# Products for the meta tokens over 128 rows, with meta tiles that are cleared once, in a hybrid retention and latent-attention encoder block

## The chip, the cores and the metric

The kernel runs on one core of a Trainium2 chip. The metric is the device time of one execution in microseconds (us). A time is quoted as the median of several executions; the profile is that of one further execution, whose own time is given beside it. The engines are TensorE (PE: its matrix products; PEld: its weight loads), VectorE (DVE), ScalarE (ACT), GpSimd (POOL) and SyncE (SP), whose queue issues all the DMAs that this text speaks of.

## The reference

16 learned meta tokens are put ahead of 1024 tokens of width 1024. One layer follows: a mixer with two branches, retention (8 heads, both directions, chunks of 128) and latent attention (8 heads, bidirectional softmax over all 1040 keys), then a dense SwiGLU network. At the end the meta positions are dropped, so that they matter only as keys, values and the first state of a scan. Cut to the two places where they enter:

```python
# retention, per head; the meta tokens fill the last 16 rows of the first chunk of 128
incr = jnp.einsum('bnjhd,jh,bnjhe->nbhde', kc, w_k, vc)       # state that a chunk adds
cross = jnp.einsum('bnihd,ih,nbhde->bnihe', qc, w_q, states_prev)
...
# attention, per head, over keys of 1024 tokens and 16 meta tokens
s = jnp.einsum('bqhd,bkhd->bhqk', qn, k_nope) + jnp.einsum('bqhr,bkr->bhqk', qr, k_rope)
p = jax.nn.softmax(s.astype(jnp.float32) * scale, axis=-1).astype(v.dtype)
return jnp.einsum('bhqk,bkhd->bqhd', p, v)
```

## The kernel before

All is float32. Where a product must be exact enough, an operand is split into a high and a low part (a cast and a subtraction), and three products high x high, low x high, high x low are added; line 137 to 139 (`mm3`) and line 217 are these products. Large projections use seven instead of eight block products (`seven`, line 185 on): a block of weights is loaded by SP, combined on POOL, cast on ACT (L209) and its low part made on DVE (L210), and used on PE (L217).

The program runs through these stages: the input projections with retention woven into them (retention lies between 300 and 520 us); the latent projections; the retention branch's output projection, whose last tiles (`ret_out`) are multiplied by gates that were stored earlier (load at L853, product at L854, store at L855); attention (from 693 to 985 us); the merge and the SwiGLU network.

The source is not the order of execution. The kernel is written straight through, and a scheduler with a timeline of its own moves instructions within each engine's queue, by what they depend on and by when a buffer comes free. A tile in on-chip memory lies at the next free address of a stack of pools. So a tile of another size shifts all later tiles of its pool and of the pools above, they then lie over other old tiles, and their first writes wait for other readers.

**Retention** (`core_pair`, `core`): for each of 8 heads the state that the meta tokens leave is one product, L651: the stationary operand `km` has 16 rows and 64 columns, the moving one, `vm`, 16 rows and 128 columns. It is in float32 and runs as two instructions. `km` is made once for a pair of heads (load L623, scaling on ACT at L625), `vm` is loaded for each head (L635). It lies between products of 128 rows.

**Attention** works on 32 units, each 256 queries of one head. A unit's scores (L137 to L139, 96 rows) go to DVE (L995) and ACT (the exponential, L997). Its probabilities are then turned on PE (L1005: 128x128, four to a bank) and written as high part `pth` (ACT, L1007) and low part `ptl` (DVE, L1008). The 16 meta keys are turned by L1013. Their high part goes to rows 0 to 15 and their low part to rows 32 to 47 of a ninth block of `pth` (L1016 on ACT, L1017 on DVE); before that POOL clears rows 0 to 47 of that block, in every unit (L1015). The tile `vt` of values holds the matching rows of the meta values, cleared once (L934). The unit's output is 16 products of 128 rows (L1035) and one of 48 rows for the meta keys (L1036). The output of a unit is worked out during the next unit, and `pth` and `ptl` have two buffers each. Between L1036 and the next unit's scores PE mostly has four or eight turns (L1005).

Before attention's first scores can run, its queries and keys are loaded (L951 to L954), and the weights `vr` of the values (L129, 512 KB), split into `vh` and `vl` (L132 on ACT, L133 on DVE), multiply the latent keys into `vt`: nine blocks of six products, shown as `o<-vh,ckh` and the like, each block evacuated by ACT (L1076) and DVE (L1077) through one of two PSUM tiles.

Of the kernel before, what the change touches and what calls it, by code (L numbers as in the profile page):

```python
# [10 lines left out]
F32R = mybir.dt.float32r  # L11
# [37 lines left out]
def build(nc, tc, A, out):  # L49
# [4 lines left out]
    def mk(pl, shape, tag, dt=F32):  # L54
        count[0] += 1
        name = f"{tag}_{count[0]}"
        n = int(np.prod(shape[1:]))
        if n % LINE == 0:
            return pl.tile(list(shape), dt, tag=tag, name=name)
        t = pl.tile([shape[0], -(-n // LINE) * LINE], dt, tag=tag, name=name)[:, :n]  # L60
        return t if len(shape) == 2 else t.rearrange("p (a b) -> p a b", b=shape[2])
# [4 lines left out]
    def sb(ctx, name, bufs=1, side=None, space=None):  # L66
        kw = {"reuse_waits": "tile"}
        if side:
            kw["side"] = side
        if space is not None:  # L70
            kw["space"] = space
            if space == DRAM:
                kw = {"space": space}
        return ctx.enter_context(tc.tile_pool(name=name, bufs=bufs, **kw))
# [177 lines left out]
    with ExitStack() as c1:  # L252
# [347 lines left out]


        cw = sb(cc, "core", 1)
        ay = sb(cc, "ay", 6)

        def core_pair(p):
            rq, rk = mk(cw, (P, S), "rq"), mk(cw, (P, S), "rk")
            load(rk, qk_d[1, p])
            load(rq, qk_d[0, p])
            kw = mk(cw, (P, NB, 2, P), "kw")
            km = mk(cw, (NM, 2, 64), "km")  # L610
            tf, tbk = mk(cw, (P, P), "tf"), mk(cw, (P, P), "tbk")
            load(tf, t_d[8 + p])
            load(tbk, t_d[12 + p])
            for g in range(2):
                ps = mk(pc, (P, 512), "mm").rearrange("p (c i) -> p c i", i=P)
                for c in range(4):
                    pe.transpose(ps[:, c, :], rk[:, (4 * g + c) * P : (4 * g + c + 1) * P], ident)
                for h in range(2):
                    hh = 2 * p + h
                    src = ps[:, :, h * 64 : h * 64 + 64]  # L620
                    act.mul(kw[:, 4 * g : 4 * g + 4, h, 0:64], src, kwf[:, hh : hh + 1])
                    dve.tensor_scalar(kw[:, 4 * g : 4 * g + 4, h, 64:128], src, kwb[:, hh : hh + 1], None, ALU.mult)
            load(km, km_d[p // 2, :, (p % 2) * P : (p % 2) * P + P].rearrange("t (h c) -> t h c", c=64))  # L623
            for h in range(2):
                act.mul(km[:, h, :], km[:, h, :], kwm[:NM, 2 * p + h : 2 * p + h + 1])  # L625
            return rq, rk, kw, km, tf, tbk

        def core(p, h, rq, rk, kw, km, tf, tbk):
            hh = 2 * p + h
            dmat = mk(cw, (P, P), "dmat")  # L630
            load(dmat, t_d[hh])
            hs = slice(h * 64, h * 64 + 64)
            v, vm = mk(cw, (P, NB, P), "v"), mk(cw, (NM, P), "vm")
            load(v, v_d[hh].rearrange("p (c e) -> p c e", e=P))
            load(vm, vm_d[hh])  # L635
            qw = mk(cw, (P, NB, P), "qw")
            rq3 = rq[hs].rearrange("p (c i) -> p c i", i=P)
            pool.tensor_mul(qw[0:64], rq3, tf[hs].unsqueeze(1).broadcast_to([64, NB, P]))
# [291 lines left out]
    with ExitStack() as c1:  # L930
        qk = sb(c1, "qk", 3)
        vp = sb(c1, "v", 1)
        vt = mk(vp, (P, NB + 1, H, P), "vt", F32R)
        pool.memset(f(vt)[0:48, NB], 0.0)  # L934
        ps_s = sb(c1, "ps_s", NS, space=PSUM)
        ps_o = sb(c1, "ps_o", NO, space=PSUM)
        ps_t = sb(c1, "ps_t", NT, space=PSUM)
# [72 lines left out]
        def turn_meta(prs, pt):  # L1010
            tm = mk(ps_t, (P, 4, P), "t")
            for s in range(2):
                pe.transpose(tm[:NM, s, :], prs[s][:, S:L], ident)  # L1013
            tmf = tm[:NM, 0:2, :].rearrange("p s i -> p (s i)")
            pool.memset(f(pt[0])[0:48, NB, :], 0.0)  # L1015
            act.copy(pt[0][:NM, NB, :], tmf)  # L1016
            dve.tensor_sub(pt[0][32:48, NB, :], tmf, f(pt[0])[:NM, NB, :])  # L1017

        def inverse(hh, qc, sums):
            sm = mk(w4, (P, 2), "sm")  # L1020
# [10 lines left out]
        def mix_values(hh, qc, pt, lb):  # L1031
            po = mk(ps_o, (P, 512), "o")
            for b in range(NB):
                for j in range(2):
                    pe.matmul(po[:, :256], vt[:, b, hh, :], pt[j][:, b, :], start=(b == 0 and j == 0), stop=False)  # L1035
            pe.matmul(po[:, :256], vt[0:48, NB, hh, :], pt[0][0:48, NB, :], start=False, stop=True)  # L1036
            ta, tb_ = mk(w2, (64, 256), "oa"), mk(w2, (64, 256), "ob")
            act.copy(ta, po[64:128, :256])
            act.copy(tb_, po[0:64, :256])
            pool.tensor_add(ta, ta, tb_)  # L1040
            hs = slice((hh % 2) * 64, (hh % 2) * 64 + 64)
            c = slice(qc * 256, qc * 256 + 256)
            if hh < H - 2:
                pool.tensor_mul(ta, ta, lb)
                store(o_d[hh // 2, hs, c], ta)
            else:
                pool.tensor_mul(o3[qc // 2][hs, (qc % 2) * 256 : (qc % 2) * 256 + 256], ta, lb)
# [40 lines left out]

        for i, (hh, qc) in enumerate(units):
            nxt = units[i + 1] if i + 1 < len(units) else None  # L1090
            pt = [mk(ptp, (P, NB + 1 - j, 256), t, F32R) for j, t in enumerate(("pth", "ptl"))]
            p = hh // 2
            if hh % 2 == 1 and p < 3:
                if qc == 0:
# [356 lines left out]
```

## Time and profile before

| what | value |
|---|---|
| time, median of 3 | 1789.69 us (1787.7 to 1791.53) |
| the profiled execution's own time, and its span | 1783.0 us, 1781.2 us |
| granted TensorE clock, mean | 0.989 |
| PE products, busy | 1718.1 us, 96% of the span |
| DVE, ACT, POOL busy | 1346.5, 861.8, 798.4 us |
| attention's product for the meta keys (L1036) | 32 instructions |
| clearing of the meta block (L1015, POOL) | 32 of 305 ns each |
| retention's product for the meta tokens (L651) | 16 instructions (8 products) |

A row of a timeline reads: start in us from the beginning of the span, duration in us, engine, line, operation, what it writes and reads, its shape (for a product rows*columns of the stationary operand and then the moving operand, rows x columns), and how many instructions the row merges; in brackets, the engine's idle time before it and what ended it. Products are pipelined and their ends are modelled, so the distance between two starts, not the duration, is what a product costs in a dense stream. A row of a view by stages reads: stretch, its length, and for PE, PEld, DVE, ACT and POOL the busy time with the number of instructions; then the granted clock, the DMA engines' share and GB/s.

### The profile page before, as it was taken

The page shows a single profiled execution, that of the slowest core. Times are in us where ns is not written, and L with a number is a line of the kernel's source. Part 1 is how long each engine was busy: PE and PEld are TensorE (multiplying, and loading weights), DVE is VectorE, ACT ScalarE, POOL GpSimd, SP SyncE. Part 2 cuts the span into 40 slices and gives each one's busy share as a digit, 9 for nine tenths or more (in the row PEclk, how much of TensorE's full clock was granted, in tenths as well). Part 3 has the DMA queues.
Part 4 walks back from the last instruction along what each step waited for, and adds up shares of the span by engine and source line. Part 5 has one row for each costly group of instructions (what it writes and reads, how often), then busy time and mean ns, then how long its engine had stood idle before and what let it go on. Part 6 is the DMA issues. An engine that isn't in the chain of part 4 may idle for free.

```text
span 1781.2 us, 26455 instructions
## 1 busy us (share of the span) xinstructions
PE 1718.1 (96%) x8804; PEld 1440.9 (81%) x8804; DVE 1346.5 (76%) x2448; ACT 861.8 (48%) x1614; POOL 798.4 (45%) x633
## 2 busy tenths in 40 slices
PE   8999999999998898999999999899999999999997
PEld 6788777888887687899998888788888888787787
DVE  8846778888788767787878657767766666987965
ACT  7425766343434524677788345432333332543435
POOL 2322267575654321234332524666677656523422
PEclk9999999999999899999999999999999999999999
DMA  7734824465647784111112745233323333854512
GB/s 260 239 103 136 284 84 136 159 225 190 209 137 250 229 292 138 28 34 40 30 51 63 244 172 164 79 101 107 112 95 101 107 101 105 281 175 129 154 57 95
DMA packets 145434, 253.60 MB, mean 142 GB/s; under 512 B 18889, under 2 KB 36738, under 8 KB 145298
## 3 DMA queue, kind: packets, MB, share of 16 engines
q1 hardware_dynamic: 145298, 251.92, 43.3%
q8 instruction: 69, 1.13, 0.3%
q14 instruction: 67, 0.55, 0.1%
HBM read 174.93 MB, written 76.85 MB: 141 GB/s over the span
## 4 chain that ended last, share of the span: by engine, by line
PE 53%; DVE 7%; DMA 3%; issue 2%; ACT 2%; SPq 0%; POOL 0%; DVEq 0%; ACTq 0%; POOLq 0%
PE mm L217 33%; PE o L1035 3%; PE mm L137 3%; PE mm L138 3%; PE mm L139 3%; PE t L1005 3%; DVE slot L154 1%; PE s L137 1%; PE s L138 1%; PE s L139 1%; DMA slot<-g_d 1%; DVE ptl L1008 1%; DVE slot L210 1%; DVE pr L995 1%; PE o L138 1%
## 5 line engine op out<-in xcount | busy, mean ns | idle before, releaser
L217 PE MATMUL mm<-slot,slot 128*128 128x512 f32 x2604 | 596.1, 390 | 9.1 <-DVE slot L210 4.0
L217 PEld LDWEIGHTS mm<-slot,slot 128*128 128x128 f32 x2604 | 488.5, 188 | 115.6 <-DVE slot L210 7.0
L209 ACT CAST slot<-slot 128x512 fp32r<-128x512 f32 (+1 forms) x413 | 246.1, 597 | 453.1 <-PE mm L217 367.9
L210 DVE TENSOR_TENSOR slot<-slot,slot 128x512 fp32r<-128x512 f32 (+1 forms) x413 | 370.4, 898 | 71.8 <-ACT slot L209 70.8
L217 PE MATMUL mm<-ht,slot 128*128 128x512 f32 x648 | 219.1, 399 | 6.9 <-DVE slot L210 3.4
L191 POOL TENSOR_TENSOR slot<-slot,slot 128x512 f32<-128x512 f32 (+1 forms) x61 | 86.7, 1421 | 218.9 <-DMA slot<-in_w_in 52.9
L217 PE MATMUL mm<-h,slot 128*128 128x512 f32 x536 | 184.5, 403 | 0.0
L207 POOL TENSOR_TENSOR slot<-slot,slot 128x512 f32<-128x512 f32 (+1 forms) x61 | 83.9, 1377 | 182.2 <-DVE slot L210 169.8
L217 PEld LDWEIGHTS mm<-ht,slot 128*128 128x128 f32 x648 | 122.0, 189 | 34.5 <-DVE slot L210 5.1
L154 DVE TENSOR_TENSOR slot<-slot,slot 128x512 fp32r<-128x512 f32 x137 | 116.2, 862 | 17.9 <-ACT slot L153 17.2
L217 PE MATMUL mm<-lt,slot 128*128 128x512 f32 x324 | 128.3, 396 | 0.0
L192 POOL TENSOR_TENSOR slot<-slot,slot 128x512 f32<-128x512 f32 (+1 forms) x61 | 85.3, 1399 | 75.9 <-DVE slot L210 71.2
L217 PEld LDWEIGHTS mm<-h,slot 128*128 128x128 f32 x536 | 101.2, 190 | 21.7 <-DVE slot L210 0.6
L153 ACT CAST slot<-slot 128x512 fp32r<-128x512 f32 x137 | 83.3, 620 | 73.1 <-DMA slot<-f_d 29.6
L995 DVE TENSOR_SCALAR_CACHE_REDUCE pr<-s,sq_c 128x384 f32<-128x384 f32 (+1 forms) x192 | 103.2, 573 | 8.3 <-PE t L1013 5.4
L217 PE MATMUL mm<-l,slot 128*128 128x512 f32 x268 | 106.6, 398 | 0.0
L139 PE MATMUL mm<-slot,slot 128*128 128x512 f32 (+1 forms) x288 | 105.4, 366 | 0.0
L138 PE MATMUL mm<-slot,slot 128*128 128x512 f32 (+1 forms) x288 | 105.3, 366 | 0.0
L137 PE MATMUL mm<-slot,slot 128*128 128x512 f32 (+1 forms) x288 | 105.2, 367 | 0.0
L1008 DVE TENSOR_TENSOR ptl<-t,pth 128x512 fp32r<-128x512 f32 x128 | 85.7, 685 | 20.0 <-ACT pth L1007 19.2
L193 POOL TENSOR_TENSOR slot<-slot,slot 128x512 f32<-128x512 f32 (+1 forms) x61 | 90.1, 1477 | 1.4
L1007 ACT CAST pth<-t 128x512 fp32r<-128x512 f32 x128 | 71.8, 580 | 25.5 <-PE t L1005 25.2
(363 smaller groups left out, 3463.2 us busy)
## 6 DMA issues: line engine op xcount, KB each, us to landing
slot<-in_w_in SPq DMA_DIRECT2D x106, 256.0 KB
f_d<-slot SPq DMA_DIRECT2D x71, 256.0 KB
slot<-f_d SPq DMA_DIRECT2D x71, 256.0 KB
slot<-in_xT SPq DMA_DIRECT2D x48, 256.0 KB
slot<-z_d SPq DMA_DIRECT2D x44, 256.0 KB
slot<-in_w_g SPq DMA_DIRECT2D x44, 256.0 KB
slot<-in_w_u SPq DMA_DIRECT2D x44, 256.0 KB
slot<-in_w_dq SPq DMA_DIRECT2D x48, 192.0 KB
```

The lines of the kernel that those rows point to most:

```text
L137: pe.matmul(ps, sh, mh, start=start, stop=False)
L138: pe.matmul(ps, sh, ml, start=False, stop=False)
L139: pe.matmul(ps, sl, mh, start=False, stop=stop)
L154: dve.tensor_sub(lo, t, f(hi))
L191: pool.tensor_add(s1, a21, a22)
L192: pool.tensor_sub(s2, s1, a11)
L193: pool.tensor_sub(a21, a21, a11)
L209: act.copy(hi, side[b])
L210: dve.tensor_sub(low, side[b], f(hi))
L217: pe.matmul(ps, sw[:, ks], sx, start=begins and q == qs[0] and i == 0, stop=q == nq - 1 and i == 2, skip_group_check=True)
L995: dve.tensor_scalar(pr[:, c], ps[:, :n], sq_c[:, qb : qb + 1], None, ALU.mult, ALU.max, accum_out=mx[:, j : j + 1])
L1008: dve.tensor_sub(pt[1][d], tp, f(pt[0])[d])
```

## The change

In retention, `km` and `vm` become tiles of 128 rows that are made once, ahead of all heads, and cleared by POOL. Loads and scaling still write their first 16 rows; L651 reads all 128. In attention, the ninth block of `pth` goes away. Two tiles `ptm0` and `ptm1` of 128 rows by 256 columns take its place; they are cleared once, are used in turn by even and odd units, and only their rows 0 to 15 and 32 to 47 are rewritten. The clearing in every unit is gone, `vt` is cleared over 128 rows instead of 48, and L1036 reads 128 rows. The added rows are zero in both operands. `pth` shrinks by the 1 KB per partition of its ninth block in each of its two buffers, and the two new tiles take as much at an earlier place in the stack.

```diff
--- before.py
+++ after.py
@@ -600,6 +600,10 @@
 
 
         cw = sb(cc, "core", 1)
+
+        km, vm = mk(cw, (P, 2, 64), "km"), mk(cw, (P, P), "vm")
+        pool.memset(km, 0.0)
+        pool.memset(vm, 0.0)
         ay = sb(cc, "ay", 6)
 
         def core_pair(p):
@@ -607,7 +611,6 @@
             load(rk, qk_d[1, p])
             load(rq, qk_d[0, p])
             kw = mk(cw, (P, NB, 2, P), "kw")
-            km = mk(cw, (NM, 2, 64), "km")
             tf, tbk = mk(cw, (P, P), "tf"), mk(cw, (P, P), "tbk")
             load(tf, t_d[8 + p])
             load(tbk, t_d[12 + p])
@@ -620,19 +623,19 @@
                     src = ps[:, :, h * 64 : h * 64 + 64]
                     act.mul(kw[:, 4 * g : 4 * g + 4, h, 0:64], src, kwf[:, hh : hh + 1])
                     dve.tensor_scalar(kw[:, 4 * g : 4 * g + 4, h, 64:128], src, kwb[:, hh : hh + 1], None, ALU.mult)
-            load(km, km_d[p // 2, :, (p % 2) * P : (p % 2) * P + P].rearrange("t (h c) -> t h c", c=64))
+            load(km[:NM], km_d[p // 2, :, (p % 2) * P : (p % 2) * P + P].rearrange("t (h c) -> t h c", c=64))
             for h in range(2):
-                act.mul(km[:, h, :], km[:, h, :], kwm[:NM, 2 * p + h : 2 * p + h + 1])
-            return rq, rk, kw, km, tf, tbk
-
-        def core(p, h, rq, rk, kw, km, tf, tbk):
+                act.mul(km[:NM, h, :], km[:NM, h, :], kwm[:NM, 2 * p + h : 2 * p + h + 1])
+            return rq, rk, kw, tf, tbk
+
+        def core(p, h, rq, rk, kw, tf, tbk):
             hh = 2 * p + h
             dmat = mk(cw, (P, P), "dmat")
             load(dmat, t_d[hh])
             hs = slice(h * 64, h * 64 + 64)
-            v, vm = mk(cw, (P, NB, P), "v"), mk(cw, (NM, P), "vm")
+            v = mk(cw, (P, NB, P), "v")
             load(v, v_d[hh].rearrange("p (c e) -> p c e", e=P))
-            load(vm, vm_d[hh])
+            load(vm[:NM], vm_d[hh])
             qw = mk(cw, (P, NB, P), "qw")
             rq3 = rq[hs].rearrange("p (c i) -> p c i", i=P)
             pool.tensor_mul(qw[0:64], rq3, tf[hs].unsqueeze(1).broadcast_to([64, NB, P]))
@@ -931,7 +934,11 @@
         qk = sb(c1, "qk", 3)
         vp = sb(c1, "v", 1)
         vt = mk(vp, (P, NB + 1, H, P), "vt", F32R)
-        pool.memset(f(vt)[0:48, NB], 0.0)
+        pool.memset(f(vt)[:, NB], 0.0)
+
+        ptm = [mk(vp, (P, 256), f"ptm{i}", F32R) for i in range(2)]
+        for t in ptm:
+            pool.memset(f(t), 0.0)
         ps_s = sb(c1, "ps_s", NS, space=PSUM)
         ps_o = sb(c1, "ps_o", NO, space=PSUM)
         ps_t = sb(c1, "ps_t", NT, space=PSUM)
@@ -1012,9 +1019,8 @@
             for s in range(2):
                 pe.transpose(tm[:NM, s, :], prs[s][:, S:L], ident)
             tmf = tm[:NM, 0:2, :].rearrange("p s i -> p (s i)")
-            pool.memset(f(pt[0])[0:48, NB, :], 0.0)
-            act.copy(pt[0][:NM, NB, :], tmf)
-            dve.tensor_sub(pt[0][32:48, NB, :], tmf, f(pt[0])[:NM, NB, :])
+            act.copy(pt[2][:NM], tmf)
+            dve.tensor_sub(pt[2][32:48], tmf, f(pt[2])[:NM])
 
         def inverse(hh, qc, sums):
             sm = mk(w4, (P, 2), "sm")
@@ -1033,7 +1039,7 @@
             for b in range(NB):
                 for j in range(2):
                     pe.matmul(po[:, :256], vt[:, b, hh, :], pt[j][:, b, :], start=(b == 0 and j == 0), stop=False)
-            pe.matmul(po[:, :256], vt[0:48, NB, hh, :], pt[0][0:48, NB, :], start=False, stop=True)
+            pe.matmul(po[:, :256], vt[:, NB, hh, :], pt[2], start=False, stop=True)
             ta, tb_ = mk(w2, (64, 256), "oa"), mk(w2, (64, 256), "ob")
             act.copy(ta, po[64:128, :256])
             act.copy(tb_, po[0:64, :256])
@@ -1088,7 +1094,7 @@
 
         for i, (hh, qc) in enumerate(units):
             nxt = units[i + 1] if i + 1 < len(units) else None
-            pt = [mk(ptp, (P, NB + 1 - j, 256), t, F32R) for j, t in enumerate(("pth", "ptl"))]
+            pt = [mk(ptp, (P, NB, 256), t, F32R) for t in ("pth", "ptl")] + [ptm[i % 2]]
             p = hh // 2
             if hh % 2 == 1 and p < 3:
                 if qc == 0:
```

In the changed kernel lines from 604 on have numbers that are higher by 3 to 7. The new tiles lie below the pool that first holds `vr`, `vh` and `vl`, so these lie 2048 bytes higher than before. That is where the change moves instructions; elsewhere the order of PE, ACT, DVE and SP stays what it was, but for a pair of neighbouring DMAs in retention and one in attention.

On SP's queue, before, the load of `vr` stands behind the loads of keys and queries of the first two heads (`k`, `q`):

```order
L954 DMA q_1444_6939<-qr_1283_6148 16x1024
L951 DMA k_1447_6942<-kr_613_3038 16x1040
L952 DMA k_1447_6942<-kr_613_3038 16x1040
L954 DMA q_1445_6940<-qr_1282_6147 16x1024
L954 DMA q_1445_6940<-qr_1284_6149 16x1024
L129 DMA vr_7082<-in_w_uv 128x1024
L951 DMA k_1600_7609<-kr_612_3037 16x1040
```

On SP's queue in the changed kernel (L856, L858, L899 and L900 are the old L853, L855, L896 and L897) it stands ahead of the last stores and loads of the gated tiles:

```order
L899 DMA qr_1271_6138<-slot_6680 128x512
L129 DMA vr_7078<-in_w_uv 128x1024
L858 DMA r_d_82<-slot_6706 128x512
L900 DMA qr_1272_6139<-slot_6679 128x512
L856 DMA slot_6807<-g_d_84 128x512
L899 DMA qr_1273_6140<-slot_6711 128x512
```

So the load moves up by 28 places. Its wait is now for a product that reads `slot_6737`, the first of the last `seven`.

On ACT, at the last casts of the output projection's weights, before:

```order
L233 COPY slot_6741<-mm_6743 128x512
L894 CAST slot_6719<-slot_6718 128x512
L209 CAST slot_6862<-slot_6737 128x512
L967 CAST k_1442_6929<-kf_6958 64x384
L967 CAST k_1446_6941<-kf_6962 64x384
L132 CAST kh_7603<-kr_7601 128x256
```

and on ACT in the changed kernel (L897 is the old L894, L974 the old L967):

```order
L233 COPY slot_6733<-mm_6735 128x512
L132 CAST vh_7080<-vr_7078 128x1024
L897 CAST slot_6711<-slot_6710 128x512
L209 CAST slot_6854<-slot_6729 128x512
L132 CAST kh_7595<-kr_7593 128x256
L974 CAST k_1434_6925<-kf_6954 64x384
```

The cast to `vh` now stands ahead of the last cast of the output projection's weights. On DVE the subtraction that makes `vl` likewise moves up, to between L234 and L235 of that last `seven`, and two L966 move behind the L854 that they led.

On PE, ahead of the first scores (`s`), before:

```order
L138 MATMUL t_6996<-cql_1274_6129,qh_6917 128x384
L139 MATMUL t_6996<-cqh_1273_6128,ql_6918 128x384
L137 MATMUL s_7042<-k_1442_6929,q_1440_6927 128x384
L137 MATMUL s_7047<-k_1442_6929,q_1440_6927 128x384
L137 MATMUL t_7010<-cqh_1269_6124,qh_6917 128x384
```

and on PE in the changed kernel, from the last of the first six value products on:

```order
L139 MATMUL o_7084<-vh_7080,ckl_1268_6125 128x512
L137 MATMUL o_7093<-vh_7080,ckh_1265_6122 128x512
L138 MATMUL o_7093<-vl_7081,ckh_1265_6122 128x512
L139 MATMUL o_7093<-vh_7080,ckl_1266_6123 128x512
L137 MATMUL o_7093<-vh_7080,ckh_1267_6124 128x512
L138 MATMUL o_7093<-vl_7081,ckh_1267_6124 128x512
L139 MATMUL o_7093<-vh_7080,ckl_1268_6125 128x512
L137 MATMUL s_7038<-k_1434_6925,q_1432_6923 128x384
L137 MATMUL s_7043<-k_1434_6925,q_1432_6923 128x384
```

Twelve value products (two of the nine blocks) have moved from behind the first scores to ahead of them.

## The prediction

> **What bounds the kernel now.** I read the page's first part, then the busy times by stage, then timelines of PE at the places that the change touches.
>
> ```profile
> PE 1718.1 (96%) x8804; PEld 1440.9 (81%) x8804; DVE 1346.5 (76%) x2448; ACT 861.8 (48%) x1614; POOL 798.4 (45%) x633
> 300.00:520.00 220.00, 218.15 (x1223) 183.60 (x1224) 183.61 (x437) 83.99 (x148) 142.99 (x95) 1.00 0.60 194
> 680.00:700.00 20.00, 14.03 (x63) 12.74 (x61) 10.50 (x19) 5.83 (x13) 6.34 (x7) 0.83 0.61 177
> 740.00:985.00 245.00, 240.55 (x1713) 222.64 (x1712) 200.20 (x601) 190.33 (x419) 85.55 (x124) 1.00 0.17 47
> ```
>
> PE is the bound. In retention it is idle for 1.85 of 220 us, in attention for 4.45 of 245 us, and DVE, the next, is busy for 83% and 82% of them. So what PE saves there, the kernel saves, until PE has to wait for DVE or ACT. POOL is busy for 35% of attention. The stretch between the two is another matter: from 680 to 700 us PE is idle for 6 us and its granted clock is 0.83.
>
> **Attention's meta product.** The distance between starts is what a product costs. One unit's last products, with the meta product of 48 rows:
>
> ```profile
> 795.46 0.28 PE L1035 MATMUL o<-ptl,vt 128*128 128x256 f32 x1
> 795.67 0.38 PE L1036 MATMUL o<-pth,vt 48*128 48x256 f32 x1
> 795.98 0.66 PE L1005 MATMUL t<-ident,pr 128*128 128x128 f32 x4
> 796.39 0.43 PE L137 MATMUL s<-k,q 96*128 96x384 f32 x1
> ```
>
> The same transition elsewhere, without it:
>
> ```profile
> 808.14 0.28 PE L1035 MATMUL o<-pth,vt 128*128 128x256 f32 x1
> 808.26 0.60 PE L1005 MATMUL t<-ident,pr 128*128 128x128 f32 x4
> 808.61 0.42 PE L137 MATMUL o<-ckh,kh 128*128 128x384 f32 x1
> ```
>
> With it: 796.39 - 795.46 = 0.93 us from the last L1035 to the scores (first fence). Without (second): 808.61 - 808.14 = 0.47 us. A product of 128 rows and 256 columns adds 808.26 - 808.14 = 0.12 us, so one of the usual form would make 0.59. The meta product costs 0.93 - 0.59 = 0.34 us more than its form with 128 rows: it starts 0.09 late, the turns after it 0.19, and the turns take 0.06 longer. Is it the row count? Products of 96 rows show nothing of the kind:
>
> ```profile
> 799.76 0.28 PE L1035 MATMUL o<-pth,vt 128*128 128x256 f32 x1
> 799.87 0.34 PE L137 MATMUL s<-k,q 96*128 96x384 f32 x1
> 800.05 0.33 PE L138 MATMUL s<-k,q 96*128 96x384 f32 x1
> ```
>
> 0.11 us into them, 0.18 us for 384 columns. After the change L1036 has exactly the form of L1035, so I price it at 0.12 us. 32 units x 0.34 = 10.9 us. Of this I take 95%, 10.3 us, since 1.8% of the stage is idle already and a faster PE meets DVE (82% busy, and 85% when 10 us are gone) a little more often. Bounds: 80%, 8.7 us, and the full 10.9.
>
> [...]
>
> The rows of L1036 wait for a cast of ACT, and what it waits for changes:
>
> ```profile
> 799.61 0.36 ACT L1016 CAST pth<-t 16x256 fp32r<-16x256 f32 x1
> L1015 POOL MEMSET pth<- x32: 302/305/306, 721.7 to 970.2; 48x256 f32 x32
> ```
>
> 32 clearings of 305 ns go, 9.8 us of POOL. POOL is 35% busy here, so I price this at nothing on the end; two clearings of a tile, `vt`'s larger one and retention's two take under 3 us of POOL by the same row (cost goes by columns: 256 take 0.3), under POOL's idle time. The cast now waits for the meta product of two units earlier to have read the tile. The meta product that ends at 796.05 is that of the unit before the cast's, so even it leaves 799.61 - 796.05 = 3.6 us, and the one that matters lies a unit further back, (970.2 - 721.7) / 31 = 8.0 us by the clearings: 11 us in all. I price it at nothing; if that cover went, every 0.1 us of wait would be 3.2 us over 32 units.
>
> **Retention's meta product.** The same comparison, two instructions of 16 rows and 64 columns against two of the same type with 128 rows and columns:
>
> ```profile
> 314.71 0.39 PE L217 MATMUL mm<-ht,slot 128*128 128x512 f32 x1
> 315.03 0.43 PE L651 MATMUL mm<-vm,km 16*64 16x128 f32 x2
> 315.39 0.50 PE L217 MATMUL mm<-h,slot 128*128 128x512 f32 x1
> ...
> 498.48 0.40 PE L217 MATMUL mm<-l,slot 128*128 128x512 f32 x1
> 498.71 0.38 PE L670 MATMUL mm<-st,qw 128*128 128x128 f32 x2
> 498.85 0.71 PE L217 MATMUL mm<-h,slot 128*128 128x512 f32 x2
> ```
>
> And one of few columns:
>
> ```profile
> 806.90 0.33 PE L139 MATMUL o<-ckh,kl 128*128 128x384 f32 x1
> 807.08 0.38 PE L1013 MATMUL t<-ident,pr 128*16 128x128 f32 x2
> 807.21 0.37 PE L1035 MATMUL o<-ptl,vt 128*128 128x256 f32 x1
> ```
>
> From the product ahead to the one behind it is 0.68 us against 0.37, so 0.31 us for each of 8 heads, 2.5 us. Here 64 columns stay, which no row of 128 rows shows. The nearest, 16 columns at 807.08, starts 0.18 us after a product of 384 columns, as any does, and lets the next one start after 0.13. So few columns alone cost nothing there; I take 2.4 us, and bound it by 0 and 2.5. POOL's two clearings of 128 columns stand ahead of the first head's products on POOL, and the first load of `km` waits for one of them: under 0.6 us, on engines that are not the bound.
>
> [...]
>
> **The way into attention.** By the order, `vr` is loaded 28 DMAs earlier, `vh` and `vl` are made earlier, and twelve value products move ahead of the first scores. What is there now:
>
> ```profile
> 686.65 0.34 PE L139 MATMUL t<-cqh,ql 128*128 128x384 f32 x1
> 692.85 0.98 PE L137 MATMUL s<-k,q 96*128 96x384 f32 x2 [5.87 <-DMA q<-qr]
> 693.63 0.52 PE L137 MATMUL t<-cqh,qh 128*128 128x384 f32 x1
> 693.95 0.52 PE L138 MATMUL t<-cql,qh 128*128 128x384 f32 x1
> 699.01 0.52 PE L139 MATMUL s<-k,q 96*128 96x384 f32 x2
> ...
> 704.88 0.39 PE L138 MATMUL o<-vl,ckh 128*128 128x512 f32 x1
> 705.11 0.39 PE L139 MATMUL o<-vh,ckl 128*128 128x512 f32 x1
> ```
>
> And after another wait of PE:
>
> ```profile
> 1615.40 2.76 PE L217 MATMUL mm<-slot,slot 128*128 128x512 f32 x11 [3.13 <-DVE slot L1315]
> ```
>
> PE waits 5.87 us for the first queries. Twelve products of 0.23 us (705.11 - 704.88) fill 2.7 us of it, and are missing later, where PE is dense: 2.7 us gained. After the hole the products come 0.32 us apart (693.95 - 693.63) instead of 0.18 (800.05 - 799.87, above), until 699.01: 6.2 us, in which PE does 13 products of 384 columns and 9 of 256. At 0.18 and 0.12 us these are 3.4 us, so 2.7 us lie in the slow clock. The idle time left is about 5.9 + 0.4 (below) - 2.7, 3.6 us. After 3.13 us of idleness eleven products of 512 columns take 2.76 us, full rate; after 5.87 the rate is half. 3.6 is nearer to the first, yet I take half of this, 1.4 us, with bounds 0 and 2.7.
>
> Against it stands what the moved load is put ahead of:
>
> ```profile
> 671.47 0.32 SPq L896 DMA_DIRECT2D qr<-slot  x1
> 696.03 0.42 SPq L129 DMA_DIRECT2D vr<-in_w_uv  x1
> 700.69 1.05 ACT L132 CAST vh<-vr 128x1024 fp32r<-128x1024 f32 x1 [0.70 <-DMA vr<-in_w_uv]
> 702.84 1.21 DVE L133 TENSOR_TENSOR vl<-vr,vh 128x1024 fp32r<-128x1024 f32 x1
> ```
>
> It now follows the store at 671.47, so is issued at 671.8; from issue to cast it takes 700.69 - 696.03 = 4.7 us, so `vh` is made from 676.5 and `vl` until 678.8. Queued behind them: on ACT the last cast of weights, on DVE the sums of the last `seven`, and behind these the gated tiles whose stores stand on SP ahead of the queries. The two L966 that DVE does later give back most of 1.2 us, and a store fewer stands ahead of the queries: I take 0.4 us of delay, with bounds 0 and 4.7 (the load's own time, if transfers collide). Together 2.7 + 1.4 - 0.4 = 3.7 us, from -2.0 to 5.4.
>
> **The sum:** 10.3 + 2.4 + 3.7 = 16.4 us. The profiled execution, 1783.0 us (span 1781.2), would become 1766.6. It lies 6.7 us under the median of the runs; taken off that, 1789.7 - 16.4 = 1773.3 us.
>
> **Rivals.**
> (a) DVE takes over in attention, and half of the 10.3 us comes: 1778.5 us. For it: 82% busy, and it feeds PE's scores and turns. Against it: PE shows only 4.45 us of waiting in 245. 12%.
> (b) The moved load costs its full 4.7 us and the clock falls as before: the transition gives -2.0 us and the whole 10.7, 1779 us. For it: ACT, DVE and SP work in order, and the gated tiles' loads run then. Against it: 16 us lie between the landing, about 676.5, and the first queries at 692.85. 12%.
> (c) The rows make no difference; what follows L1036 costs its time because turns follow products. Then the 3.7 us of the transition are all, 1786.0 us. Against it: the turns at 808.26 follow a product too, without delay. 6%. [...]
> (d) Slower: the wait that takes the clearing's place. If ACT's cast into a meta tile has to wait for the meta product that last read it, then ACT's later casts of turns wait too, and PE behind them. It decides once that product slides by more than those 11 us against the cast; it outweighs the sum from 0.5 us a unit on, and at 0.8 us, 25.6 in all, the kernel takes 1798.9 us. For it: two tiles only, rewritten in turn. Against it: the 11 us, and `pth` had two buffers as well. 3%.
>
> **Chances.** My forecast 67%, the rivals 12, 12, 6 and 3. A measurement of this kernel can hardly tell less than 0.2%, 3.6 us. (a), (b) and the forecast are faster by more; (c) lies at that bound and is shared, 2 and 4; (d) is slower. Faster 93%, same 4%, slower 3%. Low end: gains of 10.9, 2.5 and 5.4 give 1770.9, less 4 for the distance of up to 6.7 us that one execution here has from a median; high end: 8.7, 0 and -2.0 give 1783.0.
>
> **What would show it.** L1036 with the form 128*128, 0.12 us after its neighbour, and 0.59 instead of 0.93 us up to the scores; attention from the first scores on shorter by about 10 us; L651 to its next product in 0.37 us; the first scores still at about 693 us, the idle time before them near 3.6 us and, if the clock holds, 0.18 us between the products after. It is wrong if L1036 keeps its delay, if PE's idle time in attention grows by as much as PE saves, or if the first scores come 3 us later.

## The result, and the profile after

The changed kernel takes 1778.75 us (median of 6 runs, 1775.05 to 1780.81) against 1787.47 us of the kernel before, run beside it (6 runs): a ratio of 0.9945, with a 95% interval of 0.9931 to 0.9960. Run a second time beside the later experiments it gave 1777.44 us and 0.9948 (0.9933 to 0.9963). In that second round one execution of the kernel before (2846.54 us) and one of the changed kernel (4370.62 us) took far longer than the others and are left out of the ratio. So it is faster, by 9 to 10 us out of the 16.4 us forecast. The 1773.3 us were only 5.4 us too low because the forecast started from 1789.7 us, the median of three earlier runs; against the kernel beside it 6.6 to 7.1 us of the gain are missing.

The stages of the changed kernel, in the same view as before (the stretch, PE, PEld, DVE, ACT and POOL busy with their instructions, granted clock, DMA share, GB/s):

```profile
300.00:520.00 220.00, 217.34 (x1209) 182.11 (x1208) 182.92 (x434) 86.84 (x152) 145.60 (x99) 1.00 0.58 193
680.00:700.00 20.00, 16.00 (x65) 13.62 (x65) 14.84 (x24) 5.47 (x10) 4.60 (x6) 0.84 0.59 194
740.00:985.00 245.00, 236.82 (x1732) 224.93 (x1731) 200.71 (x604) 190.59 (x420) 77.46 (x97) 1.00 0.18 53
```

Attention is the row to look at. Its window is the same 245 us, which now reach past the stage's end: PE is busy for 3.7 us less in it than before, and some of that is idle time inside the stage. The meta product itself does what was forecast. One unit's last products, PE's timeline of the changed kernel:

```profile
794.57 0.28 PE L1041 MATMUL o<-ptl,vt 128*128 128x256 f32 x1
794.68 0.28 PE L1042 MATMUL o<-ptm,vt 128*128 128x256 f32 x1
794.80 0.60 PE L1012 MATMUL t<-ident,pr 128*128 128x128 f32 x4
795.16 0.42 PE L137 MATMUL s<-k,q 96*128 96x384 f32 x1
```

L1042 (the old L1036) has the form 128*128, starts 0.11 us after its neighbour, and the scores follow 795.16 - 794.57 = 0.59 us after the last L1041, where it was 0.93. As much, 0.33 to 0.39 us, is gone behind 31 of the 32 meta products. And yet this unit is no shorter. What PE waits for between the first and the last meta product, first before, then after (engine, operation, who was waited for: us in total, times, longest):

```profile
PE o L1035 <- ACT pth L1007: 2.5, 5, 1.5
...
PE t L1013 <- DVE ptl L1008: 0.3, 1, 0.3
```

```profile
PE o L1041 <- ACT pth L1014: 3.7, 6, 1.8
PE t L1020 <- DVE ptl L1015: 2.1, 7, 0.3
```

The turn of the meta columns (L1020, the old L1013) waits for DVE's low parts 7 times instead of once, 0.3 us each. One of the seven, like the one before, lies near the end of the stage (at 968.18 and 972.22 us); the other six are new. Retention shows no gain at all. PE's timeline of the changed kernel at the first head's meta product (L654, the old L651):

```profile
318.90 0.39 PE L217 MATMUL mm<-ht,slot 128*128 128x512 f32 x1
319.22 0.43 PE L654 MATMUL mm<-vm,km 128*64 128x128 f32 x2
319.58 0.50 PE L217 MATMUL mm<-h,slot 128*128 128x512 f32 x1
```

319.58 - 318.90 = 0.68 us, as before with 16 rows. The way into attention, from the first product for keys to the first product with probabilities, on PE of the kernel before:

```profile
672.97 0.33 PE L137 MATMUL t<-ckh,kh 128*128 128x384 f32 x1
...
723.92 0.39 PE L1035 MATMUL o<-pth,vt 128*128 128x256 f32 x1 [2.25 <-ACT pth L1007]
```

And on PE, SP and ACT of the changed kernel:

```profile
677.51 0.38 SPq L129 DMA_DIRECT2D vr<-in_w_uv  x1
...
678.86 0.33 PE L137 MATMUL t<-ckh,kh 128*128 128x384 f32 x1
...
681.59 1.05 ACT L132 CAST vh<-vr 128x1024 fp32r<-128x1024 f32 x1 [0.81 <-DMA vr<-in_w_uv]
...
694.38 0.66 PE L137 MATMUL t<-cqh,qh 128*128 128x384 f32 x1 [3.27 <-DVE kf L973]
...
697.39 0.63 PE L137 MATMUL o<-vh,ckh 128*128 128x512 f32 x1
697.82 0.63 PE L138 MATMUL o<-vl,ckh 128*128 128x512 f32 x1
...
701.52 0.51 PE L137 MATMUL s<-k,q 96*128 96x384 f32 x2
...
724.59 0.39 PE L1041 MATMUL o<-pth,vt 128*128 128x256 f32 x1 [1.87 <-ACT pth L1014]
```

The values' weights come early, and twelve value products stand ahead of the first scores, as the order said. PE's hole is 3.27 us long, where 3.6 was forecast. The clock falls all the same: the granted clock is 0.50 from 695 to 700 us, and the value products come 697.82 - 697.39 = 0.43 us apart, not 0.23. From the first key product of the stage to the first product with probabilities it is 724.59 - 678.86 = 45.73 us; before it was 723.92 - 672.97 = 50.95, with the same 192 products.

But the hole isn't the one of before, made shorter. The value products don't fill it: they all come behind it. So do the nine products that make the first queries (`t<-cqh,qh`, from 694.38 us), which in the kernel before stood ahead of the hole (the last of them at 686.65). PE now waits for DVE's `kf` instead of the queries. DVE before, then in the changed kernel:

```profile
679.33 1.13 DVE L966 TENSOR_TENSOR kf<-t,skv_b 64x384 f32<-64x384 f32 x2
...
686.51 1.70 DVE L854 TENSOR_TENSOR slot<-slot,slot 128x512 f32<-128x512 f32 x1 [3.83 <-DMA slot<-g_d]
```

```profile
692.49 0.69 DVE L857 TENSOR_TENSOR slot<-slot,slot 128x512 f32<-128x512 f32 x1 [3.49 <-DMA slot<-g_d]
693.10 1.13 DVE L973 TENSOR_TENSOR kf<-t,skv_b 64x384 f32<-64x384 f32 x2
```

The two L966 (now L973) that moved back in DVE's queue wait there behind a product with a gated tile that isn't loaded yet. The wait for the queries is gone: 21 products now lie between the hole and the first scores.

That gives three questions. Why does attention give half? Is retention's price the 64 columns? And is the way in worth 5 us, or is that one execution?

### The profile page after: what moved, and what is told of

Same layout as the page of the kernel before. It is cut to its first block, busy times and chain, and to the rows that moved or that the text cites. A ratio compares the mean times of both kernels' runs of the same rounds, so it can differ in the third digit from the quotient of the medians.

```text
span 1779.0 us, 26433 instructions
## 1 busy us (share of the span) xinstructions
PE 1714.6 (96%) x8804; PEld 1443.9 (81%) x8804; DVE 1339.0 (75%) x2448; ACT 861.1 (48%) x1614; POOL 790.1 (44%) x605
## 4 chain that ended last, share of the span: by engine, by line
PE 49%; DVE 7%; DMA 3%; ACT 3%; issue 2%; SPq 0%; POOL 0%; DVEq 0%; ACTq 0%; POOLq 0%
PE mm L217 29%; PE o L1041 3%; PE mm L138 3%; PE mm L137 3%; PE mm L139 3%; PE t L1012 2%; DVE slot L154 2%; PE s L137 1%; PE s L138 1%; PE s L139 1%; DMA slot<-g_d 1%; DMA slot<-f_d 1%; DVE slot L210 1%; DVE ptl L1015 1%; PE o L137 1%
## 5 line engine op out<-in xcount | busy, mean ns | idle before, releaser
L210 DVE TENSOR_TENSOR slot<-slot,slot 128x512 fp32r<-128x512 f32 (+1 forms) x413 | 361.6, 877 | 71.5 <-ACT slot L209 70.4
L1046 POOL TENSOR_TENSOR oa<-oa,ob 64x256 f32<-64x256 f32 x32 | 24.0, 751 | 154.5 <-ACT ob L1045 149.1
```

The source lines that it names most:

```text
L210: dve.tensor_sub(low, side[b], f(hi))
```

## Experiments: the parts apart

All ratios are to the kernel before, run beside them, with 95% intervals.

**Attention without retention.** The retention part is undone:

```diff
-        km, vm = mk(cw, (P, 2, 64), "km"), mk(cw, (P, P), "vm")
-        pool.memset(km, 0.0)
-        pool.memset(vm, 0.0)
...
+            km = mk(cw, (NM, 2, 64), "km")
...
+            v, vm = mk(cw, (P, NB, P), "v"), mk(cw, (NM, P), "vm")
```

> The changed kernel with the retention part of the change undone: km has 16 rows and vm has 16 rows, nothing is cleared there; attention is as in the change. Theory (the product with 64 columns keeps its price whatever its rows, so retention gave nothing): the time of the change, 1778.8 us, and 0.68 us from the product ahead of the meta product of retention to the one behind it. Rival (retention gave the 2.4 us of the prediction, and attention gave less): 1781.2 us.

Measured: 1777.36 us, 0.9932 (0.9917 to 0.9947). It is no slower than the whole change. Retention's part gave nothing.

**128 columns as well.**

```diff
-        km, vm = mk(cw, (P, 2, 64), "km"), mk(cw, (P, P), "vm")
+        km, vm = mk(cw, (P, 2, P), "km"), mk(cw, (P, P), "vm")
...
-            pe.matmul(u0[:64, :P], km[:, h, :], vm, start=True, stop=True)
+            pe.matmul(u0[:, :P], km[:, h, :], vm, start=True, stop=True)
```

> The changed kernel, and retention's meta product gets 128 columns as well (km has 128 columns per head, the upper 64 zero; what they give is not read). Theory (it was the 64 columns that kept the price): 0.37 instead of 0.68 us from the product ahead to the one behind, 8 times 0.31 = 2.5 us less, 1776.3 us. Rival (the price is that of 16 used rows, or PE there waits for other engines so that nothing comes of it): 1778.8 us.

Measured: 1774.74 us, 0.9924 (0.9910 to 0.9937), about 3.8 us less than the change by the two ratios, whose intervals still overlap. The trace is sharper. PE at the second head:

```profile
345.35 0.39 PE L217 MATMUL mm<-ht,slot 128*128 128x512 f32 x1
345.58 0.38 PE L654 MATMUL mm<-vm,km 128*128 128x128 f32 x2
345.72 0.48 PE L217 MATMUL mm<-lt,slot 128*128 128x512 f32 x1
```

0.37 us in place of 0.68. From the second to the eighth head's meta product it is 515.28 - 345.58 = 169.70 us, in the change 518.52 - 347.12 = 171.40: 1.7 us by the trace. Five of the eight heads show 0.37 or 0.38, two 0.45 and 0.56 (0.56 and 0.80 with 64 columns), and the first 1.02, where the profile has PE waiting for 0.42 us. It was the columns: at this head it is 0.68 us with 16 rows and 64 columns, 0.69 with 128 rows and 64 columns, and 0.37 with 128 of both. What PE does in the 0.31 us between, no run shows.

**48 rows in the changed kernel.** All instructions stand in the order of the change, on every engine:

```diff
-            pe.matmul(po[:, :256], vt[:, NB, hh, :], pt[2], start=False, stop=True)
+            pe.matmul(po[:, :256], vt[0:48, NB, hh, :], pt[2][0:48], start=False, stop=True)
```

> The changed kernel, but attention's meta product reads 48 rows of both operands again; the two cleared tiles, their place in memory and the order on all engines stay. Theory (the rows are worth 5 us in attention, since one kind of unit meets a loop through ACT, DVE and PE of 7.45 us and gains nothing; the rest of the gain comes from the way into attention): 1784 us, units with four turns behind the meta product again 7.45 us, those with eight 7.30 instead of 6.97 us. Rival (the rows are worth the predicted 10.3 us and something else was lost): 1789 us. Rival (rows are worth nothing, all is layout): 1778.8 us.

Measured: 1784.14 us, 0.9968 (0.9956 to 0.9980). So 5.7 us of the gain stay without the rows, and the rows are worth about 4 us by the ratios. By the trace, from the first to the last meta product it is 250.97 us, against 245.76 in the change and 250.48 before: 5.2 us, half of the 10.3. This also prices the clearings: they are gone here, and attention is as long as before. Taking 9.8 us from POOL was worth nothing, as forecast.

**The tiles above the value weights.** The two tiles go to a pool that opens after the value weights are done with, so that these lie where they lay:

```diff
-        ptm = [mk(vp, (P, 256), f"ptm{i}", F32R) for i in range(2)]
-        for t in ptm:
-            pool.memset(f(t), 0.0)
...
         ptp = sb(c1, "pt", 2)
+        pmt = sb(c1, "ptm", 1)
+        ptm = [mk(pmt, (P, 256), f"ptm{i}", F32R) for i in range(2)]
+        for t in ptm:
+            pool.memset(f(t), 0.0)
```

> The changed kernel, but the two meta tiles lie above the value weights, in a pool opened after these are done with; so the value weights lie where they lay before, and their load and the twelve value products stand in the order of before. Rows are 128. Theory (the way into attention is worth 4 to 5 us of the gain): 1783 us, first scores and the hole ahead of them as before (5.9 us of idleness). Rival (the way in is worth nothing, the gain is all from the rows): 1778.8 us.

Measured: 1781.56 us, 0.9962 (0.9949 to 0.9976). PE's timeline of this kernel, to be set beside the change's rows above:

```profile
675.50 0.33 PE L137 MATMUL t<-ckh,kh 128*128 128x384 f32 x1
...
694.35 0.98 PE L137 MATMUL s<-k,q 96*128 96x384 f32 x2 [5.07 <-DMA q<-qr]
...
725.41 0.39 PE L1037 MATMUL o<-pth,vt 128*128 128x256 f32 x1 [2.25 <-ACT pth L1010]
```

The hole of over 5 us is back, it ends with the queries again, and the stage takes 725.41 - 675.50 = 49.91 us. The attention behind it is that of the change (245.57 us from the first to the last meta product). In the ten profiles of kernels with the tiles below, this stretch takes 44.65 to 46.48 us, in the two with the old place 50.95 and 49.91. So the way in is worth 3.4 to 6.3 us by the traces, with about 5 in the middle, and 3.0 us by the two ratios. No cost hides ahead of the stretch that stands out from the scatter: from retention's last meta product to its start the ten take 157.8 to 161.3 us, the two 159.2 and 159.3.

## Experiments: why attention gave half

The distances between starts of neighbouring meta products tell it (us, read from the starts; counted from the first meta product):

| unit | before | change | 48 rows | 48 rows in block 2 | 48 rows in block 6 | copies later | sum on DVE | sum on DVE, 48 rows |
|---|---|---|---|---|---|---|---|---|
| 22, eight turns behind the meta product | 7.31 | 6.98 | 7.31 | 7.33 | 7.36 | 6.97 | 6.95 | 7.31 |
| 15, four turns behind it | 7.45 | 7.45 | 7.43 | 7.83 | 7.46 | 6.96 | 6.95 | 7.29 |
| 18, next heads' keys and queries are made | 10.08 | 10.16 | 10.16 | 10.15 | 10.13 | 9.57 | 9.47 | 9.65 |
| first to last of the 32 | 250.48 | 245.76 | 250.97 | 257.30 | 253.12 | 240.60 | 239.01 | 246.52 |

From before to the change, 13 distances (like 22) give 4.42 us together, from 0.19 to 0.62, 0.34 each on average: the full price. The six like 15 (6 to 8, 14 to 16) give 0.00, the six like 18 (2, 3, 10, 11, 18, 19) lose 0.04, the last six give 0.30. At 0.34 each, these three groups of six miss 2.0, 2.1 and 1.7 us. So it isn't that each unit gives half; some give all and others nothing.

The units of 7.45 us run in a loop of exactly that length. ACT, DVE and PE of the changed kernel, one turn of it:

```profile
785.96 0.60 PE L1012 MATMUL t<-ident,pr 128*128 128x128 f32 x4
786.59 0.59 ACT L1014 CAST pth<-t 128x512 fp32r<-128x512 f32 x1 [0.70 <-PE t L1012]
787.08 1.16 ACT L1004 ACTIVATE pr<-pr,nm 128x1040 f32<-128x1040 f32 x1
...
788.34 0.37 ACT L1044 COPY oa<-o 64x256 f32<-64x256 f32 x1
788.73 0.37 ACT L1045 COPY ob<-o 64x256 f32<-64x256 f32 x1
789.00 0.58 ACT L1014 CAST pth<-t 128x512 fp32r<-128x512 f32 x1
789.61 0.69 DVE L1015 TENSOR_TENSOR ptl<-t,pth 128x512 fp32r<-128x512 f32 x1 [0.75 <-ACT pth L1014]
790.36 0.39 PE L1020 MATMUL t<-ident,pr 128*16 128x128 f32 x2 [0.29 <-DVE ptl L1015]
...
793.41 0.60 PE L1012 MATMUL t<-ident,pr 128*128 128x128 f32 x4
794.05 0.59 ACT L1014 CAST pth<-t 128x512 fp32r<-128x512 f32 x1 [0.70 <-PE t L1012]
```

Four turns on PE (785.96) let ACT cast (786.59). Behind the cast ACT's queue holds the exponential, the two copies of the last unit's output and the next cast (789.00). DVE makes the low part from that (789.61). This frees PSUM for the turn of the meta columns (790.36), for which PE waits 0.29 us. PE then works without a gap up to the next unit's four turns (793.41), and ACT's cast follows at 794.05: 794.05 - 786.59 = 7.46 us. The meta product (787.23 us) isn't part of it: it runs while ACT and DVE have the turn of the loop. The kernel before shows that the loop was closed already. DVE and the weight load of the meta turn (PEld) there, and PEld's wait in sum:

```profile
790.52 0.69 DVE L1008 TENSOR_TENSOR ptl<-t,pth 128x512 fp32r<-128x512 f32 x1 [0.75 <-ACT pth L1007]
791.26 0.10 PEld L1013 LDWEIGHTS t<-ident,pr 128*16 128x16 f32 x2 [0.15 <-DVE ptl L1008]
...
PEld t L1013 <- DVE ptl L1008: 1.5, 7, 0.5
```

PE's products had no gap there, and yet the turn started only 0.05 us after the low part was done. Six of these seven waits of PEld lie in the six units.

If that is right, PE time taken or added where the meta product stands changes nothing, and PE time added between 790.36 and 793.41 lengthens the unit by all of it.

**48 rows inside the loop.** A product with 48 rows is put among the products behind the meta turn, and, as a control, among the last seven. "Drain" is here only a name for the 0.34 us that such a product cost at the meta keys. Both kernels leave out 80 of the 128 keys of one block; the order of instructions stays that of the change:

```diff
-                    pe.matmul(po[:, :256], vt[:, b, hh, :], pt[j][:, b, :], start=(b == 0 and j == 0), stop=False)
+                    r = slice(0, 48 if (b, j) == (2, 0) else P); pe.matmul(po[:, :256], vt[r, b, hh, :], pt[j][r, b, :], start=(b == 0 and j == 0), stop=False)
```

The control has `(6, 0)` in place of `(2, 0)`.

> The changed kernel, but one of attention's 16 value products per unit, that of the high parts of key block 2, reads 48 of its 128 rows (it leaves out 80 keys of that block; this costs no time by itself). So a change of the row count costs PE 0.34 us again, but in front of the turns, not at the meta product. Theory (units with four turns run in a loop PE - ACT - DVE - PE of 7.45 us, which holds the products from the turn of the meta columns to the next four turns, and not the last seven and the meta product): here the drain lies inside the loop, so these units take 7.45 + 0.34 = 7.79 us; first to last meta product 245.8 + 32 times 0.33 = 256 us, 1789 us in all. Rival (PE merely has 0.29 us to spare in these units, wherever the drain lies): 7.45 to 7.50 us as in the run with 48 rows of the meta product, 251 us, 1784 us.

> As the run before, but the product of 48 rows is that of the high parts of key block 6 (80 keys of that block are left out), among the last seven ahead of the meta product, which by the theory lie outside the loop. The order on all engines is that of the changed kernel. Theory: 7.45 us for units with four turns, first to last meta product 251 us, 1784 us, like the run with 48 rows of the meta product. Rival (the place makes no difference): as the product in block 2 gives.

Measured: block 2, 1788.89 us, 1.0002 (0.9991 to 1.0012); block 6, 1785.80 us, 0.9982 (0.9972 to 0.9993). The same 48 rows, a few products apart, and 7.83 or 7.84 us against 7.43 to 7.46 in each of the six units. That leaving out keys costs no time by itself was an estimate; the runs give the price of such a product only as a whole. PE with the 48 rows in block 2, then in block 6:

```profile
789.14 0.39 PE L1020 MATMUL t<-ident,pr 128*16 128x128 f32 x2 [0.29 <-DVE ptl L1015]
789.81 0.38 PE L1041 MATMUL o<-pth,vt 48*128 48x256 f32 x1
793.86 0.28 PE L1042 MATMUL o<-ptm,vt 128*128 128x256 f32 x1
796.98 0.39 PE L1020 MATMUL t<-ident,pr 128*16 128x128 f32 x2 [0.30 <-DVE ptl L1015]
```

```profile
790.53 0.39 PE L1020 MATMUL t<-ident,pr 128*16 128x128 f32 x2
...
794.45 0.38 PE L1041 MATMUL o<-pth,vt 48*128 48x256 f32 x1
...
797.96 0.39 PE L1020 MATMUL t<-ident,pr 128*16 128x128 f32 x2
```

Inside the loop PE still waits its 0.29 us, 796.98 - 789.14 = 7.84 us later; outside it the wait is used up (no bracket at L1020) and the unit keeps its length, 797.96 - 790.53 = 7.43 us. The loop holds. (The control's whole attention is 2 us longer than forecast, 253.12 us, through distances 11, 19, 20 and the last ones.)

**Taking the copies out of the loop.** Two ways, both with 128 columns in retention. In the first, a unit's two output copies are issued after the next cast:

```diff
-            act.copy(ta, po[64:128, :256])
-            act.copy(tb_, po[0:64, :256])
+            with tc.issue_after(casts[-2].ins):
+                act.copy(ta, po[64:128, :256])
+                act.copy(tb_, po[0:64, :256])
```

(Shown in short: `casts` collects ACT's casts of turns, and the copies move into a function of their own, which is called after both halves' turns.) In the second, one copy and POOL's addition become one addition on DVE:

```diff
             act.copy(ta, po[64:128, :256])
-            act.copy(tb_, po[0:64, :256])
-            pool.tensor_add(ta, ta, tb_)
+            dve.tensor_add(ta, ta, po[0:64, :256])
```

> The changed kernel with 128 columns in retention's meta product, and ACT's two copies of a unit's output are kept behind the next cast of turns (they are issued after it), so that they leave the loop. The planner then lays the units of four turns out with eight turns in a row as well. Theory (the loop through ACT was what kept 0.34 us a unit): the six units of 7.45 us in heads 1 and 3 go to about 7.0 us, 2.7 us in all, first to last meta product 243 us, and with the 3.8 us that the columns gave, 1772 us. Rival (DVE, busy for 85% there, sets these units): they stay at 7.4 us, 1774.7 us.

> The changed kernel with 128 columns in retention's meta product, and in attention the second copy of a unit's output and POOL's addition are replaced by one addition on DVE that reads PSUM: ACT loses 0.37 us a unit, DVE gets 0.41 us. The planner lays the units out with eight turns in a row here too. Theory (the loop through ACT): units of 7.45 us fall to about 7.0 us, 1772 us, as with the copies later. Rival (DVE sets them): DVE's 6.3 us of work a unit become 6.7, and units take 7.5 us or more, also those that took 6.97, 1776 us or more.

Measured: copies later 1772.98 us, 0.9907 (0.9891 to 0.9924); sum on DVE 1767.18 us, 0.9879 (0.9864 to 0.9894), the fastest kernel here. The distances of 7.45 us become 6.95 to 6.98 in both, and those like 18 fall too, from 10.16 to 9.57 and 9.47. DVE as the bound is out. Attention of the kernel with the sum on DVE:

```profile
740.00:985.00 245.00, 241.00 (x1754) 230.66 (x1753) 217.82 (x640) 186.26 (x392) 63.33 (x72) 1.00 0.22 63
```

DVE has more to do than ever (217.82 us in this window, which here reaches past the end of attention, against 200.71) and the units are shorter. No full engine was in the way: the loop was, and it is gone. Both edits also let the scheduler lay these units out with eight turns in a row, so whether the copies' new place or the new layout broke it isn't told apart. Against the run with 128 columns alone, attention is 5.0 and 6.6 us shorter (from 245.59 us), and the whole by the ratios 3.0 and 8.0 us.

**The rows without the loop.** The last check: with the loop gone, are the rows worth their full price?

> The kernel with the addition on DVE (units of 7.45 us gone, 128 columns in retention), and attention's meta product reads 48 rows again; order and places are the same. Theory (the loop through ACT is all that kept half of the gain of the rows): without the loop the rows are worth their full 0.33 us in every unit, so first to last meta product goes from 239.0 to 249 to 249.6 us, and the time from 1767.2 to 1778 us. Rival (a part is kept by something else, as DVE, which is busier here): 244 us and 1772 us, the half that the changed kernel showed.

Measured: 1776.20 us, 0.9941 (0.9926 to 0.9957): 11 us slower than with 128 rows by the two ratios, each uncertain by 2.7 us. By the trace it is 246.52 - 239.01 = 7.5 us, between the two theories. The six units of 7.45 us now show it in full (7.29 to 7.31 against 6.95 to 6.98, 2.0 us together); of the six like 18 only 0.7 us comes. So the loop kept 2 us of what was missing. With it gone 3 us of 31 x 0.34 = 10.5 are missing still: 1.4 in the six like 18, 0.8 in the three that follow them (4, 12 and 20), and 0.8 in the last six. In those like 18 of the changed kernel PE's gaps are small; the clearest sits behind the eight turns of distance 2, where the profile names no wait. PE and DVE there:

```profile
746.71 0.62 DVE L1002 TENSOR_SCALAR_CACHE_REDUCE pr<-s,sq_c 128x384 f32<-128x384 f32 x1
...
747.13 0.27 PE L1029 MATMUL t<-ident,sm 128*2 128x128 f32 x1
747.38 0.44 PE L137 MATMUL s<-k,q 96*128 96x384 f32 x1
```

The scores start 0.25 us after the short turn ahead of them (0.03 before), when DVE, late from the new keys (L973), has read the score tile that they need. That DVE's queue sets this is read from the times, and wasn't tried by a run of its own. What holds the last six units wasn't tried either.

**The change once more.**

> The changed kernel as it is, once more, beside the run above, to tell its ratio better. Theory (5 us from the rows, 4 to 5 from the way into attention, nothing from retention): 0.9945 to 0.995 of the time of before, 1778 to 1779.5 us; first to last meta product 245.8 us. Rival (the first runs were off and the parts add up to the 12.5 us that they gave one by one): 0.993, 1775.5 us.

Measured: 1777.44 us, 0.9948 (0.9933 to 0.9963), 245.48 us from the first to the last meta product, 44.65 us for the way in. It confirms the first result. The parts run one by one, 5.7 us without the rows and 6.8 without the way in, add up to more than the whole only within their intervals of 2.1 to 2.5 us each way.

## Why the prediction was right or wrong

- **Faster, and in the range: right.** By its parts, read from traces: 4.7 us from attention, 5 us from the way in, 0 from retention. That is 9.7 us, and the two ratios give 9.8 and 9.3. That the range held owes something to luck: two terms missed by 8.0 us together, and the third gave more than its share.
- **The price of the meta product, 0.34 us each: right:** 0.59 us came where 0.93 had been. Rival (c), by which rows make no difference, falls with this and with the run of 48 rows.
- **"32 units x 0.34 ..., of this I take 95%": the step that failed,** by 5.6 us. The 1.8% of idle time and DVE's 85% are averages over a stage whose units differ. A loop through ACT, DVE and PE already lasted exactly as long as PE's own work in six units (7.45 us both), and the meta product lies outside it. An average cannot show that; the row that could was that of the weight loads, PEld's seven waits for DVE's `ptl` in the kernel before. Of the 10.5 us of 31 full prices 5.8 are missing, and the loop is shown for 2.0 of them. 2.1 us are missing in the six units like 18, where DVE's queue is the likely cause, and 1.7 us in the last six; these causes stay open. The bound of 80% was not low enough either.
- **Rival (a)** gave 1778.5 us, the time that came, with 12%. Half of its mechanism is there: PE came to wait for others and half of the sum was lost. But DVE did not take over by being full: in the six units it waits for ACT (0.75 us in the loop above), and they became shorter when DVE got more to do. That the forecast of this rival meets the measured time so closely is chance, since retention and the way in came out otherwise than it has them.
- **Retention, 2.4 us: wrong,** 0 us came. The row with 16 columns that the price was taken from did not stand for 64: with those the 0.68 us stayed. The bound of 0 held.
- **The way into attention, 3.7 us: faster, as forecast, but not by the path forecast.** "Twelve products of 0.23 us ... fill 2.7 us of it" failed: none of them runs in the hole. The two L966 that were to give back most of 1.2 us made a hole of their own, behind a gated tile's load. That it is 3.27 us long, with 3.6 forecast, is luck. What holds of the forecast is that the wait for the queries gets covered, by 21 products behind the hole. The gain comes from the tiles' place, as the run with the tiles above shows (3.4 to 6.3 us); what each moved instruction gives wasn't tried apart. The moved load cost little: from its issue to the cast it took 681.59 - 677.51 = 4.1 us, and rival (b), a net loss of 2.0 us, falls with the net gain. The term for the clock came only in part. In the execution shown it fell for as long as before (0.84 and 0.83 from 680 to 700 us); in six of the ten profiles with the new way in it shows 0.91, and these take 44.65 to 45.05 us against 45.51 to 46.48 in the other four. The term for the fill was too small, since the later waits went as well: the five ahead of the first product with probabilities in the kernel before (0.17, 0.43, 0.20, 0.19 and 2.25 us) became one of 1.87. First scores came at 701.5 us, not 693: about 6 us of the shift lie ahead of the stage in this execution, the rest comes with the hole's new place and the twelve products, seven of which are followed by the next 0.42 or 0.43 us later, not 0.23.
- **POOL's clearings at nothing: right** (the run with 48 rows). **Rival (d)** didn't occur: ACT's 32 casts into the meta tiles waited for the turn of the meta columns alone, 4 times and 2.3 us in all.

## What to carry to other kernels

Before a saving on a busy engine is multiplied by its count, the chain that closes each kind of unit has to be followed through the other engines' queues: a unit can be as long as its loop and as PE's work at once, and then only the loop's members pay. The weight loads' waits can show such a loop while the products show no gap. Where a short copy stands in a queue ahead of the cast that frees the bottleneck, an edit that takes it out of the way can be worth as much as the saving was: here, together with the new layout that came of it, attention became 5.0 and 6.6 us shorter, and by the rows 4.7 us. Padding the product to full rows paid here only where the columns were full as well: 4.7 us by the trace in attention with 128 columns, nothing in retention with 64 (0.68 us before and after).

## What the runs showed of the hardware

The runs show a price for some forms of a product, and it is not one for each row: 48 of 128 rows cost 0.34 us at the meta product, and 0.35 to 0.38 us a unit among the value products, whichever block is cut (7.33 and 7.36 against 6.98 in units like 22); 128 rows with 64 columns cost the same 0.31 us as 16 rows with 64, for two instructions in a row. Products of 96 rows show no such price: with 384 columns they start 0.17 or 0.18 us apart (796.66 to 797.36 us in the kernel before), as those of 128 rows do (806.03 to 806.90 us). What PE does in those 0.31 to 0.38 us, no run shows.

A hole in PE's work of 2.9 to 3.3 us was followed by a lower granted clock in each of the ten profiles with the new way in (0.84 or 0.91 from 680 to 700 us, or 0.86 or 0.93 from 680 to 705), as one of 5.9 us had been before (0.51 from 692 to 699 us), while the one of 3.13 us late in the kernel before was not (1.00 from 1615 to 1620 us). At the same late place the change's first profile has a hole of 3.06 us (up to 1612.31 us), and a granted clock of 0.72 over the next 5 us. Behind the hole of the new way in, the time at half rate comes in two sizes. From 680 to 700 us the change's first profile, shown above, has a granted clock of 0.84; its second has:

```profile
680.00:700.00 20.00, 16.76 (x74) 14.20 (x74) 14.62 (x23) 6.96 (x13) 5.63 (x7) 0.91 0.56 177
```

If the clock there is either full or half (single microseconds show 1.00 and 0.50), 0.84 over 20 us is an estimated 6.4 us at half rate, 0.91 an estimated 3.6 us: the same kernel, with holes of 3.27 and 3.24 us. Why holes of one length fare differently, no run shows. The executions also differ by up to 4 us in their first 60 us, before any changed instruction (PE's 201st instruction starts between 60.38 and 64.44 us); that is why stages were compared here and not only sums.
